# Two queues and two banks: an encoder trunk whose residual stores move to ScalarE's queue and whose output projection uses four PSUM banks in its second half

## The chip, the cores and the metric

The kernel runs on one core of a Trainium2 chip, in one launch. Times are microseconds (us) of device time for one execution. The engines of the core each work through an instruction stream of their own, in order: PE (TensorE, matrix products), DVE (VectorE), ACT (ScalarE), POOL (GpSimd) and SP (SyncE, which here does nothing but start transfers). An instruction that waits for another engine holds up everything behind it on its own engine. PSUM, into which PE writes its products, has eight banks; each holds one 128 x 512 tile in float32.

## The reference

A bidirectional encoder trunk with two layers, on one sequence of 1024 tokens of width 1024, all in float32. With what matters here kept:

```python
for l in range(DEPTH):                       # 2
    mod = (silu(c) @ w_mod[l] + b_mod[l])    # six vectors sh1, sc1, g1, sh2, sc2, g2
    h = rms_norm(x, norm_g[l, 0]) * (1 + sc1) + sh1
    # four groups of heads on h @ w_in[l]: windowed, short convolution, latent, dilated
    y = concatenate([oa, ob, oc, od]) @ w_out[l]          # the output projection
    x = x + g1 * rms_norm(y, norm_g[l, 1])                # residual
    h = rms_norm(x, norm_g[l, 2]) * (1 + sc2) + sh2
    u = dwconv3(h @ w_up[l], ffn_conv[l])                 # the up projection
    ug, uv = split(u)
    y = (gelu(ug) * uv) @ w_down[l]
    x = x + g2 * rms_norm(y, norm_g[l, 3])                # residual
```

## The kernel before

Activations are kept transposed: a tile is 128 features by 1024 tokens, and eight tiles (`y[0]` to `y[7]`) make the width of 1024. The tokens are worked on in two halves of 512 (`HALVES`), so that one half's norms can run beside the other half's matmuls. Products keep float32 accuracy by splitting each operand into a rounded high part and a rest, and adding three products: high by high, high by rest, rest by high (`mm3`, L465, and `product`, L472). One tile of an output for one half is eight input tiles times three matmuls of 128 x 128 by 128 x 512, 24 matmuls in all, summed in one PSUM bank.

**PSUM.** Three pools share the eight banks (L1252): `pj` with two banks, `psc` with two, and `po` with two buffers of two banks. A tile asked of a pool gets one of its banks once what was in it has been read.

**The output projection** (`project_out`, L1076). Its first half is computed as four tiles at once, in the banks of `pj` and `psc` (L1108), and then four more one after another in `pj` (L1111). Then `between[0]` is traced, the residual of the first half. The second half's eight tiles follow in the order 2, 3, 4, 5, 0, 1, 6, 7, each in a bank of `pj` (L1114); after tile 0 comes `between[1]`, which normalises the new first half for the feed-forward part. ScalarE copies each finished tile out of PSUM (L1104). PE goes on with the up projection of the first half (L1127, also in `pj`). The second half's residual and its norm run beside that.

**The residual** (`residual`, L449). First `rstd` (L146) computes the reciprocal root mean square over the eight tiles: ScalarE squares each tile (L164), some squares are summed on VectorE or GpSimd (L171), PE sums over partitions by a product with ones (L158), and VectorE does the root (L176 to L191). Then, tile by tile: the old x is loaded, two tiles to a transfer (L457, on SP's queue); VectorE scales y (L460); VectorE adds x for even tiles and GpSimd for odd ones (L461); and the new x is stored (L462). All these stores go to a tensor `xd` in HBM, from which the next residual loads x, except those of the last residual, which write the output. `modulated` (L433) then needs a second `rstd`, now over the new x, and writes the high part (ScalarE, L442) and the rest (VectorE, L447, or GpSimd, L445) of the normalised half.

The residual runs twice in each layer behind the output projection (`token_half`, L1297) and twice at each layer's end (`layer_end`, L1309), there beside the second half of the down projection (L1168 adds that product into y) or the next layer's first products.

**What sets the order.** The code is traced in program order, and a planner then deals the instructions out to the engines: each engine takes, at the time that the planner reckons with, the earliest traced instruction that it reckons ready. The order on each engine is fixed after that, and so is that in each queue of transfers. SP's queue carries nearly all loads: weights (L116), x (L457), the modulation weights (L357), and the stores of the residual.

Of the kernel before, what the change touches and what calls it, by code (L numbers as in the profile page):

```python
# [92 lines left out]
class Trunk:  # L93
# [355 lines left out]
    def residual(self, y, l, g, hs, xsrc, dst, temp, adders=None, rs=None):  # L449

        nc, w = self.nc, hs.stop - hs.start
        rs = rs or self.rstd([t[:, hs] for t in y], D, temp, adders)
        for k in range(KT):
            yk = y[k][:, hs]
            if k % 2 == 0:
                xs = temp("x")[:, :2 * w]
                nc.sync.dma_start(xs.rearrange("p (a f) -> p a f", a=2),  # L457
                                  xsrc[128 * k:128 * k + 256, hs].rearrange("(a p) f -> p a f", a=2))
            x = xs[:, w * (k % 2):w * (k % 2) + w]
            nc.vector.scalar_tensor_tensor(yk, yk, self.col(l, g, k), rs, op0=ALU.mult, op1=ALU.mult)  # L460
            (nc.gpsimd if k % 2 else nc.vector).tensor_add(yk, yk, x)  # L461
            nc.sync.dma_start(dst[128 * k:128 * k + 128, hs], yk)  # L462


    def mm3(self, ps, wh, wl, xh, xl, first, last):  # L465
# [610 lines left out]
    def project_out(self, l, y, between):  # L1076
        nc = self.nc
        order = ORDER_MIX
        with self.tc.tile_pool(name=f"wo{l}", bufs=1, reuse_waits="tile") as wo:
            def load(m, eng=None):  # L1080
                at = (None, ("wh", "wl")) if m < 2 else (self.fw, ("uh", "ul")) if m < 6 else (wo, (f"oh{m}", f"ol{m}"))
                return self.weight(self.a["w_out"][l, m], 1024, *at, eng=eng)

            ws = [load(m) for m in range(2)]
            for k in order:
                n = 64 if k == 5 else 128
                nc.sync.dma_start(self.hl[k][0:n].bitcast(F32), self.mixd[128 * k:128 * k + n, :])
            for half in range(2):
                hs = HALVES[half]
                for k in order:  # L1090
                    n = 64 if k == 5 else 128
                    self.split(self.hh[k][0:n, hs], self.hl[k][0:n, hs], self.hl[k][0:n, hs].bitcast(F32))
            ws += [load(m, nc.vector) for m in range(2, 4)]

            def products(half, ms, pools, turns):
                hs = HALVES[half]
                ps = [pool.tile([128, 512], F32, name="pw", tag=tag) for pool, tag in pools]
                for i, k in sorted(((i, k) for i in range(len(ms)) for k in order),
                                   key=lambda t: order.index(t[1]) if turns else t[0]):
                    w, ks = ws[ms[i]], slice(128 * k, 128 * k + 128)  # L1100
                    self.mm3(ps[i], w[0][:, ks], w[1][:, ks], self.hh[k][:, hs], self.hl[k][:, hs],
                             k == order[0], k == order[-1])
                    if k == order[-1]:
                        nc.scalar.activation(y[ms[i]][:, hs], ps[i], AF.Copy)  # L1104

            pj, psc = (self.pj, "pj"), (self.psc, "psc")

            products(0, range(4), (pj, pj, psc, psc), True)  # L1108
            ws += [load(m) for m in range(4, 8)]
            for m in range(4, 8):  # L1110
                products(0, (m,), (pj,), False)  # L1111
            between[0]()
            for m in (2, 3, 4, 5, 0, 1, 6, 7):
                products(1, (m,), (pj,), False)  # L1114
                if m == 0:
                    between[1]()

# [281 lines left out]
```

## Time and profile before

| | |
|---|---|
| median of three runs | 3243.86 us (3236.26 to 3246.94) |
| the profiled execution's own time | 3236.76 us |
| its span, first to last instruction | 3234.9 us |
| granted TensorE clock, mean | 0.974 of full speed |
| PE busy | 2985.9 us, 92% |
| VectorE busy | 2029.7 us, 63% |
| ScalarE busy | 1063.9 us, 33% |
| GpSimd busy | 956.7 us, 30% |
| bytes moved | 237.15 MB, 73 GB/s on average |

An engine's busy time is the sum over its instructions. Starting a transfer isn't counted as busy. Matmuls are pipelined: one takes about 0.39 us from start to end, but the next starts 0.23 us after it. In the timelines a bracket at the end of a row gives the idle time of the engine just before that instruction, and the instruction whose end released it.

### The profile page before, as it was taken

The page shows a single profiled execution, that of the slowest core. Times are in us where ns is not written, and L with a number is a line of the kernel's source. Part 1 is how long each engine was busy: PE and PEld are TensorE (multiplying, and loading weights), DVE is VectorE, ACT ScalarE, POOL GpSimd, SP SyncE. Part 2 cuts the span into 40 slices and gives each one's busy share as a digit, 9 for nine tenths or more (in the row PEclk, how much of TensorE's full clock was granted, in tenths as well). Part 3 has the DMA queues.
Part 4 walks back from the last instruction along what each step waited for, and adds up shares of the span by engine and source line. Part 5 has one row for each costly group of instructions (what it writes and reads, how often), then busy time and mean ns, then how long its engine had stood idle before and what let it go on. Part 6 is the DMA issues. An engine that isn't in the chain of part 4 may idle for free. (4 is left out here: it accounts for less than half of the span.)

```text
span 3234.9 us, 35358 instructions
## 1 busy us (share of the span) xinstructions
PE 2985.9 (92%) x13706; PEld 2365.9 (73%) x13706; DVE 2029.7 (63%) x2849; ACT 1063.9 (33%) x1554; POOL 956.7 (30%) x712
## 2 busy tenths in 40 slices
PE   7888988988999999999988998898899999999997
PEld 3677767776677777788856886777676888888886
DVE  6687567698656666653587727568956434434347
ACT  4232443554332222212243324336534222222222
POOL 1221133324342322223232213142334422233222
PEclk9998999999999999999999998999999999999998
DMA  5235111103312433211131121110132111111113
GB/s 202 78 101 177 54 37 34 56 20 108 128 58 93 134 113 114 95 40 52 46 124 58 55 82 42 38 52 19 37 109 91 65 39 40 43 62 52 40 40 104
DMA packets 103091, 237.15 MB, mean 73 GB/s; under 512 B 11227, under 2 KB 29915, under 8 KB 102924
## 3 DMA queue, kind: packets, MB, share of 16 engines
q1 hardware_dynamic: 102924, 234.90, 22.4%
q8 instruction: 107, 1.75, 0.2%
q14 instruction: 60, 0.49, 0.1%
HBM read 205.59 MB, written 32.67 MB: 74 GB/s over the span
## 5 line engine op out<-in xcount | busy, mean ns | idle before, releaser
L111 POOL TENSOR_TENSOR wl<-raw,wh 128x1024 fp32r<-128x1024 f32 (+2 forms) x96 | 234.5, 2451 | 663.7 <-ACT wh L110 472.4
L477 PE MATMUL pj<-hp,uh 128*128 128x512 f32 x880 | 352.6, 401 | 1.6 <-ACT hp L442 1.6
L478 PE MATMUL pj<-hp,uh 128*128 128x512 f32 x880 | 347.1, 394 | 2.9 <-POOL hp L445 2.8
L477 PE MATMUL pj<-hh,wh 128*128 128x512 f32 x800 | 327.9, 410 | 14.2 <-DVE ql L526 8.5
L478 PE MATMUL pj<-hl,wh 128*128 128x512 f32 x800 | 323.2, 404 | 3.7 <-POOL hl L445 3.2
L481 PE MATMUL pj<-hp,ul 128*128 128x512 f32 x880 | 290.2, 394 | 0.0
L111 POOL TENSOR_TENSOR ul<-raw,uh 128x1024 fp32r<-128x1024 f32 x96 | 238.5, 2486 | 162.5 <-PE pj L481 84.7
L875 DVE TENSOR_SCALAR ta<-u,par 128x1024 f32<-128x1024 f32 (+1 forms) x46 | 55.9, 1216 | 356.1 <-ACT u L1128 324.0
L477 PE MATMUL pj<-hx,uh 128*128 128x512 f32 x528 | 212.5, 403 | 12.6 <-ACT u L1128 10.0
L110 ACT ACTIVATE wh<-raw 128x1024 fp32r<-128x1024 f32 (+2 forms) x104 | 107.2, 1047 | 345.1 <-PE po L469 242.8
L481 PE MATMUL pj<-hx,ul 128*128 128x512 f32 x528 | 209.8, 397 | 0.0
L478 PE MATMUL pj<-hx,uh 128*128 128x512 f32 x528 | 207.7, 393 | 0.0
L481 PE MATMUL pj<-hh,wl 128*128 128x512 f32 x800 | 206.5, 398 | 0.0
L477 PEld LDWEIGHTS pj<-hp,uh 128*128 128x128 f32 x880 | 165.6, 188 | 45.6 <-ACT hp L442 2.2
L478 PEld LDWEIGHTS pj<-hp,uh 128*128 128x128 f32 x880 | 165.5, 188 | 44.9 <-POOL hp L445 5.5
L481 PEld LDWEIGHTS pj<-hp,ul 128*128 128x128 f32 x880 | 165.2, 188 | 39.3 <-issue 1.0
L477 PEld LDWEIGHTS pj<-hh,wh 128*128 128x128 f32 x800 | 154.4, 193 | 54.0 <-issue 17.0
L110 ACT ACTIVATE uh<-raw 128x1024 fp32r<-128x1024 f32 x100 | 105.5, 1059 | 262.9 <-DMA raw<-in_w_up_dram 141.2
L1190 DVE TENSOR_TENSOR y<-y,po 128x1024 f32<-128x1024 f32 x96 | 117.0, 1219 | 110.6 <-PE po L470 110.6
L478 PEld LDWEIGHTS pj<-hl,wh 128*128 128x128 f32 x800 | 154.1, 193 | 41.8 <-POOL hl L445 5.4
L481 PEld LDWEIGHTS pj<-hh,wl 128*128 128x128 f32 x800 | 151.6, 190 | 34.6 <-issue 0.2
L1128 ACT ACTIVATE u<-pj 128x512 f32<-128x512 f32 x176 | 103.7, 593 | 209.1 <-PE pj L481 209.1
(375 smaller groups left out, 7120.2 us busy)
## 6 DMA issues: line engine op xcount, KB each, us to landing
raw<-in_w_up_dram SPq DMA_DIRECT2D x88, 512.0 KB, 3.5
mr<-in_w_mod_dram SPq DMA_DIRECT2D x144, 256.0 KB, 3.4
raw<-in_w_in_dram SPq DMA_DIRECT2D x52, 512.0 KB, 3.5
raw<-in_w_down_dram SPq DMA_DIRECT2D x44, 512.0 KB, 3.5
room<-in_w_mod_dram SPq DMA_DIRECT2D x48, 256.0 KB, 3.6
xd<-y SPq DMA_DIRECT2D x48, 256.0 KB, 2.4
raw<-in_w_out_dram SPq DMA_DIRECT2D x16, 512.0 KB, 3.9
x<-xd SPq DMA_DIRECT2D x14, 512.0 KB, 4.4
```

Source lines behind the costliest of these rows:

```text
L110: self.nc.scalar.activation(hi, src, AF.Copy)
L111: (eng or self.nc.gpsimd).tensor_sub(lo, src, hi.bitcast(F32))
L477: nc.tensor.matmul(ps, wh[:, ks], self.hh[k][:, hs], start=k == 0, stop=False, skip_group_check=True)
L478: nc.tensor.matmul(ps, wh[:, ks], self.hl[k][:, hs], start=False, stop=False, skip_group_check=True)
L481: nc.tensor.matmul(ps, wl[:, ks], self.hh[k][:, hs], start=False, stop=k == KT - 1, skip_group_check=True)
L875: nc.vector.tensor_scalar(o, t[:, 0:n], cw(0), None, op0=ALU.mult)
L1128: nc.scalar.activation(u[:, 1 + 512 * half:513 + 512 * half], ps, AF.Copy)
L1190: self.mark = nc.vector.tensor_add(d, d, p)
```

## The change

Two lines. In `residual`, the store of each tile is issued by ScalarE and no longer by SP, unless it goes to the output. In `project_out`, the tiles of the second half take their banks from `pj` for odd tile numbers and from `psc` for even ones; so their order 2, 3, 4, 5, 0, 1, 6, 7 alternates between the two pools.

```diff
@@ -459,7 +459,7 @@
             x = xs[:, w * (k % 2):w * (k % 2) + w]
             nc.vector.scalar_tensor_tensor(yk, yk, self.col(l, g, k), rs, op0=ALU.mult, op1=ALU.mult)
             (nc.gpsimd if k % 2 else nc.vector).tensor_add(yk, yk, x)
-            nc.sync.dma_start(dst[128 * k:128 * k + 128, hs], yk)
+            (nc.sync if dst is self.a["out"] else nc.scalar).dma_start(dst[128 * k:128 * k + 128, hs], yk)
@@ -1111,7 +1111,7 @@
                 products(0, (m,), (pj,), False)
             between[0]()
             for m in (2, 3, 4, 5, 0, 1, 6, 7):
-                products(1, (m,), (pj,), False)
+                products(1, (m,), (pj if m % 2 else psc,), False)
                 if m == 0:
                     between[1]()
```

## Rows read from the trace of the kernel before

**Rows 1.** The page's first part: busy time, share of the span, instructions.
```profile
PE 2985.9 (92%) x13706; PEld 2365.9 (73%) x13706; DVE 2029.7 (63%) x2849; ACT 1063.9 (33%) x1554; POOL 956.7 (30%) x712
```

**Rows 2.** PE's waits, whole run: waiter, released by, us in total, times, longest.
```profile
PE pw L468 <- ACT y L1104: 2.8, 2, 1.4
PE pj L477 <- ACT y L1104: 2.6, 2, 1.3
...
PE po L158 <- ACT sq L164: 8.5, 9, 1.7
...
PE po L158 <- DVE ta L171: 5.6, 3, 4.5
```

**Rows 3.** Table by stage: stretch, us, busy times, granted clock, DMA share, GB/s.
```profile
core 0: us, PE busy (x) PEld busy (x) DVE busy (x) ACT busy (x) POOL busy (x), PEclk, DMA share, GB/s
825.00:850.00 25.00, 25.00 (x108) 19.95 (x107) 18.37 (x27) 9.92 (x15) 11.85 (x7) 1.00 0.59 200
...
1630.00:1640.00 10.00, 8.76 (x39) 6.87 (x38) 10.00 (x12) 2.51 (x4) 4.01 (x3) 1.00 0.81 274
1640.00:1660.00 20.00, 15.12 (x37) 7.26 (x35) 17.15 (x28) 11.54 (x18) 9.33 (x7) 0.83 0.51 185
```

**Rows 4.** Timeline of PE: start, us, line, operands, [idle before, releaser].
```profile
846.91 1.02 PE L158 MATMUL po<-ta,ones 128*128 128x512 f32 x2
...
860.47 0.50 PE L468 MATMUL pw<-hx,oh 128*128 128x512 f32 x1 [1.36 <-ACT y L1104]
...
867.62 0.50 PE L477 MATMUL pj<-hx,uh 128*128 128x512 f32 x1 [1.31 <-ACT y L1104]
...
870.58 2.97 PE L158 MATMUL po<-sq,ones 128*128 128x512 f32 x6 [0.82 <-ACT sq L164]
...
1646.17 2.04 PE L158 MATMUL po<-ta,ones 128*128 128x512 f32 x2 [4.53 <-DVE ta L171]
```

**Rows 5.** Timeline of VectorE, layer 0's token stage.
```profile
841.62 0.69 DVE L171 TENSOR_TENSOR ta<-ta,tc 128x512 f32<-128x512 f32 x1 [0.32 <-ACT tc L164]
...
893.21 1.02 DVE L461 TENSOR_TENSOR y<-y,x 128x512 f32<-128x512 f32 x1 [1.91 <-DMA x<-in_x_dram]
```

**Rows 6.** Timeline of ScalarE, layer 0's token stage and end.
```profile
859.84 0.58 ACT L1104 ACTIVATE y<-pw 128x512 f32<-128x512 f32 x1
...
866.99 0.58 ACT L1104 ACTIVATE y<-pw 128x512 f32<-128x512 f32 x1
...
868.91 0.58 ACT L1104 ACTIVATE y<-pw 128x512 f32<-128x512 f32 x1
869.39 0.62 ACT L164 ACTIVATE acc<-y 128x512 f32<-128x512 f32 x1
...
1682.53 0.63 ACT L164 ACTIVATE sq<-y 128x512 f32<-128x512 f32 x1 [0.43 <-POOL y L461]
```

**Rows 7.** Timeline of GpSimd, layer 0's token stage and end.
```profile
869.08 1.28 POOL L445 TENSOR_TENSOR hp<-tn,hp 128x512 fp32r<-128x512 f32 x1
...
883.43 1.66 POOL L461 TENSOR_TENSOR y<-y,x 128x512 f32<-128x512 f32 x1 [8.83 <-DVE y L460]
...
1629.36 1.68 POOL L461 TENSOR_TENSOR y<-y,x 128x512 f32<-128x512 f32 x1 [1.29 <-DVE y L460]
...
1638.19 1.30 POOL L461 TENSOR_TENSOR y<-y,x 128x512 f32<-128x512 f32 x1 [4.19 <-DMA x<-xd]
```

**Rows 8.** Timeline of SP's queue: first issue, us from first to last, count.
```profile
885.12 0.81 SPq L462 DMA_DIRECT2D xd<-y  x2
885.97 0.45 SPq L457 DMA_DIRECT2D x<-in_x_dram  x1
...
1629.91 4.44 SPq L462 DMA_DIRECT2D xd<-y  x4
1634.39 0.46 SPq L457 DMA_DIRECT2D x<-xd  x1
```

**Rows 9.** The stores' line: one issue in ns (min/median/max), first and last start.
```profile
L462 SPq DMA_DIRECT2D xd<-y x48: 319/320/432, 828.1 to 2475.8; - x48
```

## The prediction

> **What bounds the kernel now.** First the page's busy times: PE is busy for 92% of the span and no other engine comes near it [rows 1]. So an edit is worth what it takes from PE's idle time, and nothing more unless it makes PE's clock rise. Second, the list of PE's waits over the whole run [rows 2]. The two lines that the bank edit can reach are the first two, matmuls (pw of the output projection, and pj, the up projection behind it) that wait for ScalarE's eviction at L1104: 2.8 and 2.6 us, two times each, once in each layer. The stores can reach the other two, the sums of squares (L158) that wait for a square (8.5 us) or for VectorE's sum of squares (5.6 us). That is 19.5 us in all, 0.6% of the span, and a bound on what can be won without the clock. Third, the table by stage [rows 3]: from 825 to 850 us, where the first half's residual runs, PE is busy 25.00 of 25 us, so nothing that happens to that residual is felt at once. Last, the timelines around the two residuals of layer 0 [rows 4 to 8]; layer 1 repeats the three waits of PE to within 0.1 us, so what follows counts twice.
>
> **The bank edit.** PE finishes tile m=1 of the second half and finds no free bank until 860.47 (1.36 us idle), and the first up product waits until 867.62 (1.31 us) [rows 4]. The evictions are late because of their place on ScalarE: that of m=6 starts at 866.99 and that of m=7 at 868.91, between the writes of the normalised first half [rows 6]. With four banks neither wait is needed: the bank that m=6 wants was emptied four tiles before, and the first up product takes a bank that the copy at 859.84 empties [rows 6]. Removed: 2.67 us a layer, 5.4 in all. Nothing is added: the eight evictions are the same.
>
> Where does PE go with it? The first up product would start at 867.62 - 2.67 = 864.95. In PE's order eight matmuls follow (867.62 to 870.58 less the wait of 0.82, with 0.23 us from one start to the next), and then the second half's first sum of squares, which today waits 0.82 us for its square at 870.58 [rows 4]. That square stands on ScalarE at 869.39, directly behind the eviction of m=7 and the normalised first half [rows 6], and the last write of that half leaves GpSimd at 869.08 + 1.28 = 870.36 [rows 7]. This chain goes back through VectorE to the sum of squares at 846.91 [rows 4, 5], before both bank waits, and PE is gapless up to there. So it doesn't move, and PE would stand before 870.58 for 870.58 - 866.9 = 3.5 us instead of 0.82: 2.7 us won and 2.7 given back. The bounds are 0 and -5.4 us over both layers. I take -1.0, near the end that the row at 870.58 speaks for, because some matmuls may be planned ahead of that sum.
>
> **The stores, on SP.** 48 stores leave SP's queue (8 a half, two halves in two layers, two more at the end of layer 0), 320 ns each [rows 9]. The 24 to the output stay. What they held up is the next load of x in the same queue. In the second half of the token stage the stores at 885.12 push a load to 885.97, whose buffer an add freed at 883.43 + 1.66 = 885.09 [rows 7, 8]; VectorE later waits 1.91 us for the last such load [rows 5]. That chain ends in PE's last waits of the stage. The load before last is 0.85 us earlier, and the last one, behind a single store, 0.4 us. Bounds 0 and -0.85 a layer; I take -0.4, twice: -0.8.
>
> At the end of layer 0 the four stores at 1629.91 to 1634.35 wait one by one for their adds, and the load of x behind them is issued at 1634.39 [rows 8]. GpSimd then waits 4.19 us for it (1638.19) [rows 7], and PE 4.53 us at 1646.17 for the sum of squares that ends this chain [rows 4]. Its buffer can be the one that the add at 1629.36 + 1.68 = 1631.04 frees [rows 7], so the load could start 3.3 us earlier. But VectorE is busy 10.00 of 10 us from 1630 to 1640 [rows 3], with work that has to be done anyway. Bounds 0 and -3.3; I take -1.0, nearer to the row of the full VectorE.
>
> The Trainium skill bears on this: "DMA: Bandwidth & Descriptors", section "Issuing engines are not separate DMA queues", says that issuing from several engines saves only the sequencer's time to start a transfer. By that alone this load would come 4 x 0.32 = 1.3 us earlier; the row at 1629.91 shows SP held for 4.44 us by four stores, most of it waiting, so I go by the row.
>
> **The stores, on ScalarE.** No row shows a DMA issued by ScalarE. Its nearest price is SP's 320 ns [rows 9]; from below it is nothing, as ScalarE is idle more than half of such a stage (9.92 of 25 us busy [rows 3]). All 48 on the path would be 15.4 us. The store of a tile and its square wait for the same add: before the last square of layer 0's end ScalarE sits idle for 0.43 us until GpSimd's add is done [rows 6]. With the store first, that square is 0.32 us later. The chain feels only the last one, since the earlier ones lie beside the next add (1.66 us on GpSimd [rows 7]). The first halves of the token stage have cover: VectorE's last sum there starts at 841.62 and takes 0.69, PE takes it up at 846.91 [rows 4, 5], 4.6 us of slack, more than 8 x 0.32 = 2.6. Four chains have none (two second halves, two at the layer's end): 4 x 0.32 = +1.3. Queued behind a waiting store are the evictions (L1104, now with two spare banks), the weight splits (L110, not needed for 10 us) and the squares.
>
> **The sum.** -1.0 - 0.8 - 1.0 + 1.3 = -1.5 us against this execution's own time of 3236.76 us (the span of 3234.9 and 1.9 around it): 3235.3. The median of the three runs is 7.1 us above it, so the forecast for a median is 3242.4; I say 3242. A difference of 0.3% (9.7 us) is about what a measurement of this kernel can tell from none.
>
> **Rivals.**
> *Nothing is given back* (0.15). The bank waits go for good (-5.4), the loads bring both bounds (-3.3 and -1.7), and with PE's pause at 1646 shortened its clock doesn't fall: the granted clock is 0.83 from 1640 to 1660, around that pause of 4.53 us, and 1.00 before it [rows 3, 4]; 20 x 0.17 = 3.4 us. In all -13.8: 3230. For it: SP visibly holds loads. Against: the chain from 846.91, and VectorE's full stretch.
> *ScalarE becomes the slow link* (0.09). In the four chains without cover each of the eight stores goes ahead of a square and costs it 0.32 us that the next add doesn't hide: 4 x 8 x 0.32 = +10.2, nothing won: 3254. It decides from three stores a chain on (3 x 4 x 0.32 = 3.8 against the 2.8 that I count as won). Against it: an add of 1.66 us leaves room for a store and the square's 0.63 [rows 6, 7].
> The Trainium skill's "Perfetto Trace Analysis", section "DMA Instruction — HWDGE (DVE, Sync)", makes this rival worse: the issuing sequencer itself waits for the semaphore and then for a block shared by both issuing sequencers. If each store also waited out one issue of SP's, the price would double by an estimate from that page, to about 20 us; no run here shows such a wait.
> *The pauses merge and the clock falls* (0.09). The pause of 3.5 us before 870.58 acts as that at 1646 did, where the granted clock fell from 1.00 (2.4 GHz) towards half (1.2 GHz) and two sums of squares took 2.04 us instead of 1.02 [rows 3, 4]. Price up to 3.4 us a layer, +6.8 - 1.5 + 1.0, as the bank gain goes with it: 3250. That pause was longer, which speaks against.
> *The loads wait for their buffers anyway* (0.07). The change then does not do for SP what its words suggest; only +1.3 - 1.0 is left: 3244.
>
> **Chances and range.** The forecast itself has 0.60. Forecast, clock and buffers lie within 9.7 us of 3243.86: same 0.76; faster 0.15; slower 0.09. The range has to reach the full gain at 3230 and the slow link at 3254, with a few us of scatter between medians inside it; 3229 to 3255.
>
> **What would show it.** Right: no wait for L1104 in front of pw or pj; a longer wait of L158 for its first square in the second halves, about 3.5 us; up products starting near 865; the load of x near 1631; the squares 0.3 us behind their adds. Wrong: the second half's squares starting well before 869, which would mean that the plan of the engines' orders itself has changed (then the bank gain stays); PE's idle time at 1646 gone, with a clock of 1.00; or evictions and squares on ScalarE standing behind a store for over a microsecond.

## The result and the profile after

The changed kernel takes 3262.32 us (median of five runs, 3257.59 to 3265.51), the one before 3239.99 (five runs, 3236.26 to 3246.94). The ratio is 1.0065 with a 95% interval of 1.0047 to 1.0082: about 21 us slower. 3242 was forecast, with 3229 to 3255.

The first part of the page and its table of queues, after (queue: packets, MB, share of 16 engines):

```profile
PE 2997.7 (92%) x13706; PEld 2372.9 (73%) x13706; DVE 2051.0 (63%) x2849; ACT 1063.8 (33%) x1554; POOL 955.5 (29%) x712
...
q10 hardware_dynamic: 6912, 12.59, 1.0%
```

ScalarE is as busy as before [rows 1], since issuing is not counted as busy. Queue q10 is new; it carries the 48 stores.

PE's waits, after, whole run:

```profile
PE po L158 <- ACT sq L164: 12.5, 8, 3.3
...
PE po L158 <- DVE ta L171: 10.8, 5, 7.3
...
PE pj L481 <- DVE wl L111: 6.3, 1, 6.3
```

No wait for L1104 is left, where 5.4 us stood [rows 2]. The sums of squares (L158) wait longer for ScalarE's squares (8.5 before) and for VectorE's sum of them (5.6 before), and a wait of 6.3 us at the layer's end has come in.

PE's timeline, after: the first half's second sum in the token stage, the first up product and the second half's first sums behind it, the sum at the layer's end, and the new wait there. A sum over one half is two matmuls in these rows (x2).

```profile
853.87 1.10 PE L158 MATMUL po<-ta,ones 128*128 128x512 f32 x2 [1.25 <-DVE ta L171]
...
871.55 0.40 PE L477 MATMUL pj<-hx,uh 128*128 128x512 f32 x1
...
876.84 5.49 PE L158 MATMUL po<-sq,ones 128*128 128x512 f32 x6 [3.28 <-ACT sq L164]
...
1660.48 2.04 PE L158 MATMUL po<-ta,ones 128*128 128x512 f32 x2 [7.33 <-DVE ta L171]
...
1696.09 2.92 PE L481 MATMUL pj<-hh,wl 128*128 128x512 f32 x6 [6.35 <-DVE wl L111]
```

Against [rows 4]: the first three sums of the second half (six matmuls) took 2.97 us behind a pause of 0.82 and now take 5.49 behind one of 3.28; the pause of 4.53 at the layer's end is now 7.33. The tables by stretch show the clock under these three sums (columns as in [rows 3]), first before, then after:

```profile
870.00:876.00 6.00, 5.42 (x14) 2.33 (x14) 0.00 (x0) 4.13 (x8) 1.78 (x4) 1.00 0.00 0
```
```profile
877.00:883.00 6.00, 6.00 (x9) 2.71 (x10) 0.00 (x0) 2.20 (x5) 1.27 (x1) 0.52 0.00 0
```

The granted clock is at its upper level before (1.00, 2.4 GHz) and close to the lower one after (0.52; 1.2 GHz is half).

ScalarE, after, in the second half of the token stage and at the end of layer 0 (ACTq: transfers that it issues; the first number is the first issue, the second the time from there to the end of the last):

```profile
894.07 0.90 ACTq L462 DMA_DIRECT2D xd<-y  x2
895.02 0.63 ACT L164 ACTIVATE sq<-y 128x512 f32<-128x512 f32 x1 [4.49 <-DVE y L460]
895.88 1.53 ACTq L462 DMA_DIRECT2D xd<-y  x2
897.45 0.63 ACT L164 ACTIVATE sq<-y 128x512 f32<-128x512 f32 x1 [1.81 <-POOL y L461]
...
1685.00 4.44 ACTq L462 DMA_DIRECT2D xd<-y  x4
1689.49 0.63 ACT L164 ACTIVATE acc<-y 128x512 f32<-128x512 f32 x1 [3.98 <-POOL y L461]
1690.93 4.38 ACTq L462 DMA_DIRECT2D xd<-y  x4
1695.36 1.67 ACT L164 ACTIVATE sq<-y 128x512 f32<-128x512 f32 x3 [5.24 <-POOL y L461]
```

The same stretch of the layer's end before, where each square starts as soon as its add is done:

```profile
1671.08 0.62 ACT L164 ACTIVATE acc<-y 128x512 f32<-128x512 f32 x1
1671.85 0.63 ACT L164 ACTIVATE sq<-y 128x512 f32<-128x512 f32 x1 [0.15 <-POOL y L461]
...
1673.67 0.63 ACT L164 ACTIVATE sq<-y 128x512 f32<-128x512 f32 x1 [0.70 <-DVE y L461]
1674.80 0.63 ACT L164 ACTIVATE sq<-y 128x512 f32<-128x512 f32 x1 [0.50 <-POOL y L461]
```

This is the main finding. The planner takes, of what it reckons ready, what was traced first, and all stores of a residual are traced ahead of the squares of the norm behind it. So two stores (token stage, and the first half of the layer's end) or four (its second half) stand ahead of a square. An issue itself is short, but ScalarE waits at each store for that tile's add: four stores hold it for 4.44 us, and the first square waits for the fourth tile. After it, 4.38 us more.

Two orders on other engines have changed with it. At the layer's end PE did the second half's sums (1672.54 to 1686.68 before) ahead of the next products with wl (L481, at 1688.13). Now six of these products stand ahead of all sums. They wait 6.35 us for wl, a weight split that VectorE does behind its eight scalings in either kernel (from 1681.29 before, 1693.76 after). The sums would not have filled that wait: the first square that PE sums (the second tile's; the first goes to GpSimd's addition) starts at 1695.36, behind the second four stores. That late squares made the plan put them last is the likely reading; the plan's reckoning itself is not on record. In the second half of the token stage GpSimd's addition of two squares (L171), which stood ahead of its last add of x (892.40 and 893.64 before), now stands behind it:

```profile
902.00 1.77 POOL L461 TENSOR_TENSOR y<-y,x 128x512 f32<-128x512 f32 x1 [2.00 <-DMA x<-in_x_dram]
905.41 1.28 POOL L171 TENSOR_TENSOR acc<-acc,sq 128x512 f32<-128x512 f32 x1 [1.63 <-ACT sq L164]
```

**A measure for it.** In each trace I took the time from VectorE's first scaling of a residual (L460) to its transposition of the second sum of squares, the one over the new x (L176). Six residuals are affected; the two first halves of the token stage were forecast to have cover, the other four not. In us:

```
                              token L0 h0, h1   layer end h0, h1  token L1 h0, h1  other four
before                          23.02  16.35       23.34  18.15      23.04  16.25        0
after                           24.52  20.40       26.18  23.86      24.44  21.04     +17.4
stores alone                    24.43  20.36       26.03  23.52      25.23  21.12     +16.9
banks alone                     23.10  16.85       23.38  19.09      23.03  16.29      +1.5
token stages alone              24.68  21.10       23.52  19.08      25.42  20.25      +9.9
layer's end alone               23.03  16.25       26.29  23.51      23.41  17.06      +9.0
own square, all                 23.11  18.43       21.82  18.14      23.03  18.53      +2.8
own square, layer's end         23.03  16.24       20.84  19.79      24.15  17.45      +0.2
behind all squares (4 banks)    23.03  16.08       22.86  19.09      23.03  16.07       0.0
on SP behind the loads          23.64  21.07       21.87  19.09      24.00  19.66      +7.6
on SP, sums on TensorE          23.62  17.15       23.79  16.65      23.65  17.14      +0.6
narrow copies                   23.03  19.05       24.40  17.90      23.15  19.03      +6.3
```

The last column is the sum over the four chains against before. Other stretches of two traces differ by some us in either direction with no chain there (5.5 us of the shift between before and after arise ahead of 190 us, where the program is the same), so the column shows the place of a loss, and the timed ratio its size. Nor is every long chain a loss: the control of experiment 11 has 18.73 and 18.63 in the second halves of the token stage, 2.4 us more each, and costs 1.6 us by its ratio.

### The profile page after: what moved, and what is told of

Read it like the earlier page. It is cut to its first block, busy times and chain, and to the rows that moved or that the text cites. A ratio compares the mean times of both kernels' runs of the same rounds, so it can differ in the third digit from the quotient of the medians.

```text
span 3263.7 us, 35340 instructions
## 1 busy us (share of the span) xinstructions
PE 2997.7 (92%) x13706; PEld 2372.9 (73%) x13706; DVE 2051.0 (63%) x2849; ACT 1063.8 (33%) x1554; POOL 955.5 (29%) x712
## 5 line engine op out<-in xcount | busy, mean ns | idle before, releaser
L481 PE MATMUL pj<-hp,ul 128*128 128x512 f32 x880 | 290.9, 395 | 0.0
L481 PE MATMUL pj<-hh,wl 128*128 128x512 f32 x800 | 210.3, 403 | 6.3 <-DVE wl L111 6.3
L481 PE MATMUL pj<-hx,ul 128*128 128x512 f32 x528 | 212.0, 401 | 0.0
L481 PEld LDWEIGHTS pj<-hp,ul 128*128 128x128 f32 x880 | 165.6, 188 | 39.9 <-issue 1.7
L481 PEld LDWEIGHTS pj<-hh,wl 128*128 128x128 f32 x800 | 153.4, 193 | 42.4 <-DVE wl L111 6.8
L637 PE MATMUL po<-s,v 128*96 128x128 f32 (+3 forms) x672 | 133.3, 361 | 44.9 <-ACT s L634 44.9
```

What stands on the lines that cost most here:

```text
L481: nc.tensor.matmul(ps, wl[:, ks], self.hh[k][:, hs], start=False, stop=k == KT - 1, skip_group_check=True)
L637: nc.tensor.matmul(o[0:96, co], v(tt, h), s[:, cs], start=co.start // 512 not in seen, stop=False, skip_group_check=True)
```

## The experiments

All were timed in five rounds against the kernel before, whose median lay between 3242.23 and 3246.96 us beside them. Microseconds are worked out from the ratio; 0.001 of it is 3.2 us. In edited kernels the line numbers move, by one to eight up or two down. Three theories stood at the start. A: the stores' place in ScalarE's order, ahead of the squares. B: the four banks, by a merged pause in which the clock falls. C: the transfers of a second queue compete with the loads.

**1. The stores alone.**
```diff
-products(1, (m,), (pj if m % 2 else psc,), False)    # the change's bank edit undone
+products(1, (m,), (pj,), False)
```


> The stores alone go to ScalarE's queue; the second half of the output projection keeps two banks. Theory A (order: the stores stand ahead of the squares in ScalarE's fixed order and make them late): +14 to +18 us against the kernel before, about 4 in each layer's second token half and 8 at the end of layer 0. Theory B (banks: PE's pauses merge in the token stage and its clock falls): the loss is mostly gone here, at most +8. Theory C (the second queue's transfers compete with the loads): +14 to +18 as for A.


3260.26 us, 1.0052 (1.0039 to 1.0065): 17 us. The stores are the cause; B falls as the main one. A and C forecast the same here.

**2. The banks alone**, the other line undone.


> The four banks alone; all stores stay on SP. The order on every engine is that of the kernel before, so only waits can differ. Theory B (the pause of PE before the second half's first sum of squares grows to about 3.5 us and its clock falls): +4 to +6 us, 2 to 3 a layer, with a granted clock under 1.00 just behind that pause. The prediction's reading (won and given back): -1, between -5 and 0, with a clock of 1.00. Theories A and C say nothing on it: 0.


3244.33 us, 1.0008 (0.9998 to 1.0017): 2.5 us, not told apart from nothing. Its PE timeline and the stretch of those sums:

```profile
870.24 0.40 PE L477 MATMUL pj<-hx,uh 128*128 128x512 f32 x1
...
876.31 5.49 PE L158 MATMUL po<-sq,ones 128*128 128x512 f32 x6 [4.04 <-ACT sq L164]
```
```profile
876.00:882.00 6.00, 5.69 (x7) 2.48 (x8) 0.00 (x0) 2.20 (x5) 1.38 (x4) 0.50 0.00 0
```

In this trace the stage begins 5.7 us later than in that of before. Less that, the up products start at 864.6 and the sum at 870.6: the first 3.1 us earlier than before, the second unmoved. The two bank waits have merged with the pause ahead of the sum, and behind the pause of 4.04 us the three sums run at a clock of 0.50.

**3. The stores on ScalarE, behind the last square** (both edits of the change kept).
```diff
+            self.due.append((dst[...], yk))                    # residual
...
+        for d, t in self.due:                                  # modulated, behind rstd
+            with self.tc.issue_after(self.square.ins):
+                nc.scalar.dma_start(d, t)
```


> Both edits, but the stores are held back on ScalarE until the last square of the new norm has been issued: as many stores on the same queue, only their place in the order differs. Theory A: the squares are as early as before, so what is left is the banks' part, 0 to +6 us against the kernel before. Theory C (transfers compete, or a store's issue costs ScalarE by itself): still +14 or more.


3259.08 us, 1.0048 (1.0036 to 1.0060). Theory A as I had put it falls: the six chains are together as short as before (one of them 0.95 longer, one 0.48 shorter), and 13 of 17 us remain beside the banks' 2.5. ScalarE, first half of the token stage:

```profile
842.57 0.63 ACT L165 ACTIVATE tc<-y 128x512 f32<-128x512 f32 x1 [1.61 <-DVE ta L172]
842.59 3.56 ACTq L441 DMA_DIRECT2D xd<-y  x5
846.20 0.60 ACT L1112 ACTIVATE y<-pw 128x512 f32<-128x512 f32 x1 [3.00 <-DMA xd<-y]
846.22 1.93 ACTq L441 DMA_DIRECT2D xd<-y  x3
```

Eight stores hold ScalarE for 5.5 us, with one eviction among them, and that eviction and the weight splits wait. The trace shows about 8 of the 13 us. In both token stages PE's pause ahead of the second half's sums is 5.71 us, 1.7 and 1.4 more than with the banks alone. At layer 0's end the squares of the second half (L165) stand behind the stores (1660.42; 1642.67 before), and PE, which before went on with their sums right after the first half's (first line, before), now waits for the normalised first half (the other lines, here):

```profile
1648.01 7.19 PE L158 MATMUL po<-sq,ones 128*128 128x512 f32 x12
```
```profile
1647.86 7.80 ACTq L441 DMA_DIRECT2D xd<-y  x7
1660.42 0.61 ACT L165 ACTIVATE sq<-y 128x512 f32<-128x512 f32 x1
...
1657.72 0.80 PE L485 MATMUL pj<-hh,wh 128*128 128x512 f32 x1 [5.19 <-ACT hh L447]
```

So the stores only change the work that waits; the rest of the 13 us was not traced.

**4. The stores on SP, behind the loads of x** (two banks; as 3, with `nc.sync.dma_start(d, t)`). No engine but SP issues anything.


> Two banks, and the stores on SP's queue, but traced behind the new norm, so that the loads of x go ahead of them. Theory A and the prediction's reading of SP's queue: the loads of x start up to 0.85 us earlier in the token stage and 3 us earlier at the end of layer 0: -1 to -4 us. If the loads wait for their buffers anyway: 0.


3253.75 us, 1.0032 (1.0020 to 1.0045): 10.5 us slower, against every theory. At the layer's end nothing is lost in the chains; the second halves of the token stage lose 4.7 and 3.4. There the loads of x run ahead of the stores in SP's queue, and GpSimd's order differs. Before (first fence) and here:

```profile
890.64 1.80 POOL L461 TENSOR_TENSOR y<-y,x 128x512 f32<-128x512 f32 x1 [2.59 <-DVE y L460]
892.40 1.28 POOL L171 TENSOR_TENSOR acc<-acc,sq 128x512 f32<-128x512 f32 x1
893.64 1.74 POOL L461 TENSOR_TENSOR y<-y,x 128x512 f32<-128x512 f32 x1
```
```profile
901.97 1.78 POOL L465 TENSOR_TENSOR y<-y,x 128x512 f32<-128x512 f32 x1 [2.03 <-DMA x<-in_x_dram]
903.71 1.26 POOL L172 TENSOR_TENSOR acc<-acc,sq 128x512 f32<-128x512 f32 x1
```

GpSimd's last add of x is now planned ahead of its addition of two squares, presumably because the last load is reckoned to come earlier. Two squares then wait for that addition ([2.79 <-POOL acc L172] in ScalarE's timeline), PE pauses for 2.55 us, and from 905 to 911 us its clock is 0.50. Theory D: the loads that run ahead turn the plan.

**5, 6. Second stores on ScalarE beside those on SP**, so that SP's queue keeps its order: 16 of 512 columns, and all of them.
```diff
+            if dst is not self.a["out"]: nc.scalar.dma_start(
+                dst[128 * k:128 * k + 128, S + 16 * (hs.start // 512):][:, :16], yk[:, :16])
```


> The kernel before, with its stores where they were (SP's queue), and beside each of the 48 a second, narrow store of the same tile, issued by ScalarE: 16 of the 512 columns, to columns of xd that nothing reads. SP's queue keeps its order, so the loads of x run as before, and hardly any bytes are added; ScalarE has as many issues ahead of its squares as in the changed kernel. Theory A (what counts is ScalarE's own time: a store is issued in ScalarE's order and what stands behind it waits): 14 to 20 us slower, the second halves' last squares about 4 us later. Theory C (the transfers of the second queue compete with the loads): 0 to 3 us. Theory D (it is the loads of x that run ahead once the stores have left SP, which turns the order on VectorE and GpSimd): 0 to 3 us.

> As the run with narrow copies, but each second store on ScalarE takes the whole 512 columns, so that 48 x 0.26 MB more are moved, on a second queue. Theory A: the same 14 to 20 us as with the narrow copies, to within 3 us. Theory C: 14 us or more, at least 10 more than with the narrow copies. Theory D: 0 to 3 us.


Narrow: 3251.61 us, 1.0023 (1.0014 to 1.0031), 7.5 us, which no theory expected. Full: 3272.33, 1.0081 (1.0067 to 1.0095), 26 us, as C would have it. An issue takes 354 and 353 ns (medians), whatever its size. With no load moved on SP and 0.40 MB added, ScalarE's issues alone cost 7.5 us, by the chains mostly in the token stages: 2.7 and 2.8 in the second halves, with GpSimd's addition ahead of its last add as before (901.18 and 902.40). At the layer's end the narrow ones lose hardly anything, and the plan puts only two of them ahead of a square there, but four of the full ones (they hold ScalarE for 4.47 us, as in the changed kernel). So A and C were not told apart cleanly: the plan's order had changed with the size.

**7. Each store behind the square of its own tile.**
```diff
             square = nc.scalar.activation(sq, t, AF.Square)
+            with self.tc.issue_after(square.ins):
+                [nc.scalar.dma_start(*self.due.pop(0)) for _ in self.due[:1]]
```


> The stores are issued by ScalarE as in the changed kernel (two PSUM banks), but each stands directly behind the square of its own tile, not ahead of the squares. A store and its square wait for the same add, so no store waits for a later add than the square in front of it; what is left is the issue time, 0.33 to 0.5 us each. Theory A: 3 to 9 us slower than before. Theory C: 14 to 18, as with the stores alone. Theory D: 10 to 14, as the loads of x run ahead here too.


3255.26 us, 1.0028 (1.0019 to 1.0037): 9 instead of 17, the upper edge of A and, by its middle, below both others (the interval, 6 to 12, reaches into D's). The same 48 issues cost 17 us ahead of the squares and 9 here, so their own time (48 x 0.326 = 15.6 us) doesn't set the loss. What is left in the second halves of the token stage, 2.1 and 2.3 us, shows the order of theory D: GpSimd's addition (901.38) stands behind its last add (899.63), and a square waits for it.

```profile
902.68 0.63 ACT L162 ACTIVATE sq<-y 128x512 f32<-128x512 f32 x1 [2.88 <-POOL acc L171]
```

GpSimd has this order in every kernel whose stores have left SP's places there (the changed one, 1, 3, 4, 7, 8). In 3 the chains are short all the same, so the order alone does not cost. In the changed kernel stores ahead of squares and this order act together: the narrow copies (2.7 and 2.8, the first alone) and this run (2.1 and 2.3, the second) come near the 4.0 and 4.9 of the stores alone when added. No run separates them inside the changed kernel.

**8. to 10. Token stages alone; layer's end alone; layer's end alone, behind the own square.**
```diff
-nc.sync.dma_start(dst[...], yk)
+(nc.scalar if g == 1 else nc.sync).dma_start(dst[...], yk)      # 8; in 9: g == 3 and not the output
```


> Only the stores of the token stages (32 of 48) are issued by ScalarE; those of layer 0's end stay on SP's queue, two banks as before. By the traces of the stores alone the two token stages lost 3.5 and 4.7 us and the layer's end 9.9. Theory A: 7 to 10 us slower, and no wait of 6 us or more at the layer's end. Theory C: two thirds of 18, about 12. Theory D: 8 to 12, as in the kernel whose stores stay on SP behind the loads, which lost nothing at the layer's end.

> Only the 16 stores of layer 0's end are issued by ScalarE, in the changed kernel's order (in the second half four stores ahead of the first square); those of the token stages stay on SP's queue, two banks. Order (a square waits for the stores ahead of it, and these for later adds): 9 to 12 us slower, the second half's sum of squares about 9 us later than before. Traffic (a second queue slows the loads): the same 9 to 12, so that this run alone does not tell the two apart; the next one does.

> As the run before it, the same 16 transfers on ScalarE's queue, but each store directly behind the square of its own tile. Order: 0 to 4 us slower, no square more than 1 us later than before. Traffic: 9 to 12 us, as with the stores ahead.


Token stages: 3252.23 us, 1.0025 (1.0015 to 1.0035), 8, where A and D both expected it. Layer's end: 3255.2, 1.0027 (1.0018 to 1.0037), 9. The two add up to the stores' 17. Layer's end behind the own square: 3247.74, 1.0011 (1.0001 to 1.0021), 3.5. ScalarE at the layer's end, second half, in that last kernel:

```profile
1683.55 0.63 ACT L162 ACTIVATE sq<-y 128x512 f32<-128x512 f32 x1 [1.19 <-DMA xd<-y]
1683.56 0.33 ACTq L164 DMA_DIRECT2D xd<-y  x1
1684.68 0.63 ACT L162 ACTIVATE sq<-y 128x512 f32<-128x512 f32 x1 [0.50 <-POOL y L461]
1684.69 0.33 ACTq L164 DMA_DIRECT2D xd<-y  x1
```

The same 16 transfers on the same queue; a store now follows its square and is issued while the square runs. With the order alone turned, 9 us became 3.5 (the two intervals just overlap, at 1.0018 to 1.0021). Seven of the eight squares of this half start less than 1 us later than before, counted from the first scaling; one is 1.5 later, against the expectation. At the layer's end, then, the order is most of the loss.

**11, 12. Theory D by itself.** In the second halves of the token stage TensorE sums all squares of the new x, so that GpSimd's addition is gone: in the kernel before (11) and in the kernel of experiment 4 (12).
```diff
-lambda: self.modulated(y, l, 2, 3, hs, t, adders[half]))
+lambda: self.modulated(y, l, 2, 3, hs, t, (nc.tensor,) if half else adders[0]))
```


> Control for the next run. The kernel before, but in the second half of the token stages all eight squares of the new x are summed by TensorE; GpSimd's one addition of two squares is gone. 0 to +2 us: eight sums instead of seven on TensorE, 0.43 us each, in two layers, less whatever GpSimd's addition held up.

> The stores on SP behind the loads (11.5 us slower before), and all squares of the second halves of the token stages summed by TensorE as in the control. Theory D in its sharper form (the loads run ahead, GpSimd's addition of two squares is then planned behind its last add of x, the squares wait for the buffers that it holds, TensorE pauses for over 3 us and its clock falls): 0 to 5 us slower than before. Rival (stores late in SP's queue hold up something else): 9 to 12 us, as without the edit.


Control: 3248.28 us, 1.0005 (0.9996 to 1.0014). With the stores behind the loads: 3252.51, 1.0019 (1.0011 to 1.0028), 6 us: 4 less than experiment 4, just outside what D expected, and 4.5 above its control. Both second halves are back at 17.1 (21.07 and 19.66 in experiment 4). D accounts for the chains of experiment 4; some 4.5 us of it stay unexplained.

**13. Own square and sums on TensorE; 14. full second stores behind the own square.**


> All 48 stores on ScalarE, each directly behind the square of its own tile, and in the second halves of the token stages all squares summed by TensorE. If what was left with the stores behind their own squares (9 us) is GpSimd's addition planned behind its last add of x: 3 to 6 us slower than before, of which 1.6 are the sums themselves. If it is the issues' own time on ScalarE, or traffic: 9 to 12 us, as without the edit.

> The stores on SP as in the kernel before, and a second, full store of every tile on ScalarE, directly behind the square of its tile (the run with full copies ahead of the squares was 26 us slower). If the order on ScalarE made that run slow: 2 to 8 us slower than before. If the doubled traffic did: 15 to 26 us, with the loads of x landing later by a microsecond or more.


13: 3257.72 us, 1.0037 (1.0024 to 1.0049), 12 us, no gain, which is what issue time or traffic would give. It doesn't decide: the plan put the first sum later (PE pauses for 3.19 us, and the three sums behind the first take 4.24 us), so the second halves grew to 21.8 for another reason. 14: 3270.17 us, 1.0069 (1.0055 to 1.0083), 22.5 us, against the order and for the traffic. VectorE there waits for x for longer than before [rows 5]:

```profile
908.03 1.78 DVE L461 TENSOR_TENSOR y<-y,x 128x512 f32<-128x512 f32 x1 [3.77 <-DMA x<-in_x_dram]
```

So with twice the bytes stored, loads of x do come late. The changed kernel adds no bytes, and its VectorE waits 0.75 us for that load (1.91 before) and starts the add 11.10 us after the first scaling (11.27 before): C is real for doubled stores, and these rows don't show it here.

No version beat the kernel before.

## Why the prediction was wrong

**What bounds the kernel** held: PE's idle time and its clock decide, and each loss ended there.

**The bank edit** (-1.0 forecast, +2.5 measured, -0.6 to 5.5). Each step of the mechanism came true: both waits gone, up products at 864.6 (864.95 said), the sum unmoved, a pause of 3.3 to 4.0 us in layer 0 (3.5 said, which is 0.82 + 2.67; the line 870.58 - 866.9 makes 3.7). The clock was priced in a rival and left out of the term. Three sums at half the clock take 2.5 us more (5.49 - 2.97), nearly the whole gain of that layer (2.67). "That pause was longer, which speaks against" was the wrong reading: the clock fell behind 3.3 us here. (The "two sums" of that rival's row at 1646 are the two matmuls of one sum.)

**The stores, on SP** (-1.8 forecast). At the layer's end the load of x did come 3.3 us earlier against its residual (1642.53 - 1636.38 = 6.15; before, from [rows 8], 1634.39 - 1624.91 = 9.48):

```profile
1642.53 0.36 SPq L457 DMA_DIRECT2D x<-xd  x1
```

Where no store stood ahead of a square, that first half gained 1.5 to 2.5 us (experiments 4, 7, 10, 13) and 0.5 (3), and lost 0.4 in one (12), so the -1.0 had mostly the right sign there. By an estimate from the page "DMA: Bandwidth & Descriptors" of the Trainium skill, section "Issuing engines are not separate DMA queues", the load would have gained 4 x 0.32 = 1.3 us; the trace shows 3.3, as the stores' waits went with them. In the token stage the sign was wrong: with the stores out of the loads' way the plan put GpSimd's addition last, there and in the changed kernel, and the chains grew by 4.7 and 3.4 in experiment 4, for -0.4 each. I had taken the order on the engines as given, and the traces show another one.

**The stores, on ScalarE** (+1.3 forecast, about 17 measured): the step that failed. It said that "the store of a tile and its square wait for the same add", that with the store first "that square is 0.32 us later", and that "the chain feels only the last one, since the earlier ones lie beside the next add". That holds for the order store, square, store, square. The order was two or four stores, then a square. What was mis-sized is not the issue (0.35 us measured, 0.32 said) but the wait: ScalarE stands at a store until that tile's add is done, so at the layer's end the first square of the second half waits for the fourth add, 3.98 us of ScalarE idle where a store was to cost 0.32. Squares "standing behind a store for over a microsecond" were named as what would show the step wrong, and that is what the trace shows. The order is shown as the cause for most of the layer's end (9 us against 3.5); in the token stage GpSimd's changed order has a part in it that no run takes out by itself. The text that says what sets the order stood ahead of the prediction, and I did not draw from it that stores, traced ahead of all squares, would win each time.

The cover of the first halves did not hold, though 4.6 us of slack were counted. Their sums come 1.4 to 1.5 us later, and PE stands idle for 1.25 and 1.18 us ahead of them (853.87 in layer 0), where it came gapless before; in the table, +17.4 without these two halves comes near the measured 21.

**The rivals.** "ScalarE becomes the slow link" had the right place, the four chains that lost most and too low a price (+10.2, from issue times alone). The Trainium skill's "Perfetto Trace Analysis", section "DMA Instruction — HWDGE (DVE, Sync)", says that the issuing sequencer itself waits for the semaphore; the trace agrees (four stores, 4.44 us). The price of about 20 us that I worked out from that page came near the result by luck: it counted a shared block, and no run here shows one. "The pauses merge and the clock falls" was right for the banks, and small.

**What stays open:** with each store behind its own square the kernel loses 9 us, against 2.8 in the chains; with all stores behind the squares some 5 of the 13 us aren't placed. In the token stage the two causes act together, and 13, meant to part them, does not.

## What to carry to other kernels

A transfer moved to an engine that computes can cost that engine its wait and not only its issue: ask what the queue of that engine will look like, instruction by instruction, and for which add the first useful instruction behind the transfers then waits. Where a planner sets the order, a change of one queue's timing can change the order on other engines, as it did on GpSimd and PE here. A wait taken from the bottleneck engine is worth something only if the next wait in its order moves too; else the pauses merge, and the clock can fall behind the longer one.

## What the runs showed of the hardware

- An issue from ScalarE took 326 to 527 ns (median 348) in the changed kernel, for 256 KB and, as narrow copies, for 8 KB alike (353 and 354). Eight behind the squares (experiment 3) held ScalarE for 5.5 us in a token stage and 8.1 at layer 0's end, single ones for up to 1.18.
- The stores landed 4.1 us after their issue on the new queue, 2.4 on SP's (medians of the page); in the changed kernel no instruction is shown waiting for one.
- A pause of PE of 2.6 to 4.0 us (experiments 2 and 4, and the changed kernel) was followed by sums of squares at a granted clock of 0.50 to 0.52, in nearly twice their time.
- VectorE's add took 1.77 us when GpSimd's had started 0.14 us ahead of it (898.78 and 898.64, after), and 0.69 when it started 0.04 us ahead of GpSimd's (890.60 and 890.64, before).
